# Forming the lower halves of weight tiles by accumulating transfers, with sums moved from GpSimd to VectorE and some casts kept in program order

## The chip, the core and the metric

The kernel runs on one core of one Trainium2 chip. The metric is the device time of one execution in microseconds (us). The engines are named as in the profile: PE is TensorE (PEld its weight loads), DVE is VectorE, ACT is ScalarE, POOL is GpSimd, SP is SyncE. An instruction waits in its engine's queue, and whatever is behind it on that engine waits with it.

## What is computed

One decoder layer on 512 tokens of width 2048, in float32. Cut to what matters:

```python
h = rmsnorm(x, norm1_g)
z = h @ w_in                       # 2048 x 5120: conv value | conv gate | q | k | v
conv_out = conformer_conv(z[..., :2048], conv_w, conv_b, conv_ln_g, conv_ln_b)
#   a * sigmoid(gate), 31 depthwise taps along the tokens, LayerNorm over 1024 channels, silu
o = diff_attention(q, k, v, lam)   # 8 heads, two 64-wide softmaxes each, their difference times v
attn_out = rmsnorm(o, subln_g) * (1.0 - lam_init)
x = x + concatenate([conv_out, attn_out]) @ w_out
h = rmsnorm(x, norm2_g)
x = x + (silu(h @ w_gate) * (h @ w_up)) @ w_down     # 2048 -> 5632 -> 2048
out = rmsnorm(x, final_g)
```

## The kernel before

**Halves.** A product of float32 matrices is made from three products of a rounded type (fp32r). Each operand a is split into an upper half, a rounded to fp32r, and a lower half, what the rounding left. `mm3` (L193 to L197) then adds upper x upper, upper x lower and lower x upper into one PSUM bank. In the profile the three products are L195, L196 and L197; for the gate and up matrices they are L666 to L668.

**Steps.** The weights come as tiles of 128 x 1024 floats (512 KB), one for each step. A step has 24 products of 512 columns. Steps 0 to 31 are the four conv groups, 32 to 47 make v, 48 to 79 are four groups of q and k, 80 to 111 are `w_out`. Then 176 steps of gate and up follow (`split_gu`, 42 products of 256 columns each, by a seven-product block scheme), and 80 steps of `w_down` with a tail. For each step `ensure` issues the load of the tile three steps ahead (tile `raw`, 3 buffers, SP's queue, L183) and the split of the tile two steps ahead.

**The split.** `split_w` calls `split` (L176 to L178): ACT copies `raw` into `wh` (L177, which rounds), and DVE subtracts, `wl` = `raw` - `wh` (L178). Both tiles have 3 buffers, so the buffer of step j is free when PE is done with step j - 3.

**Work beside the steps.** A list `at` holds what is called at the start of a given step (attention: `scores`, `transpose_a`, `attend` and `transpose_o` for 8 heads over steps 56 to 87, and `mix_split`, which splits a tile of the mixed output). `later(n, f)` enters f there, n steps ahead. A queue `bg` holds pieces of DVE work with a price each, the 31 conv taps per channel tile above all; each step earns a credit (`STEP_US` = 4.6 for the narrow steps), the price of other DVE work is taken from it (`split_w` takes 1.15), and pieces of `bg` are issued while it lasts. A scheduler then orders the instructions of each engine by its own estimate; calls wrapped in `keep` stay in program order among themselves.

**Sums.** `add_sum` (L338) adds the eight conv tiles, and `ln_center` squares on ACT (L172) and adds on POOL through `add_square` (L173); all squares share one buffer `sq`. `wout_post` adds the residual (L562) and at once issues a POOL store of it to DRAM (L563).

**From gate and up to down.** `gu_post` empties seven PSUM banks (ACT copies at L678 to L684, DVE at L679 to L683). The product of both is kept in DRAM and comes back by POOL transfers (`reload_hid`, L731); `split_hid` (L736, L737) then casts and subtracts it. The tiles of block 0 lie in slots named b, those of block 1 in slots named a. The first `w_down` step needs the banks that `gu_post` empties.

Of the kernel before, what the change touches and what calls it, by code (L numbers as in the profile page):

```python
# [10 lines left out]
F32R = mybir.dt.float32r  # L11
I32 = mybir.dt.int32
AF = mybir.ActivationFunctionType
# [3 lines left out]
P = 128  # L17
# [19 lines left out]
MIX0 = 80  # L37
STEP_US, GU_STEP_US = 4.6, 5.0
LN_WAIT = 3

C_G1, C_G2, C_GF, C_CB, C_LG, C_LB, C_SG, C_CW = 0, 16, 32, 48, 56, 64, 72, 73
NPAR = C_CW + CT * CK
# [3 lines left out]
def decoder_layer(ctx: ExitStack, tc, xT, w_in, w_out, w_gu, w_dn, par, lamv, out):  # L46
# [14 lines left out]
    def r32(ap):  # L61
        return ap.bitcast(F32)
# [120 lines left out]
        nc.sync.dma_start(t, src)  # L183
        return t

    def split_w(t):
        wh = wts.tile([P, 1024], F32R, tag="wh", bufs=3, name="wh")
        wl = wts.tile([P, 1024], F32R, tag="wl", bufs=3, name="wl")
        split(wh, wl, t)
        credit[0] -= 1.15  # L190
        return wh, wl

    def mm3(acc, ah, al, bh, bl, first, last):  # L193
# [11 lines left out]
    def later(n, f):  # L205

        at[now[0] + n].append(f)
# [90 lines left out]
    def conv_post(g):  # L298
        def post(accs):
            credit[0] -= 3.6  # L300
            value, gate = [], []
            for i in range(2):
                value.append(slotB((36 if g < 3 else 8) + 2 * g + i))
                nc.vector.tensor_tensor(value[i], accs[i], rB[0], op=ALU.mult)
            for i in range(2):
                gate.append(slotB(24 + i))
                nc.vector.tensor_tensor(gate[i], accs[2 + i], rB[0], op=ALU.mult)
                nc.scalar.activation(gate[i], gate[i], AF.Sigmoid)
            for i in range(2):
                ct = 2 * g + i  # L310
                av = value[i]
                nc.vector.tensor_tensor(av, av, gate[i], op=ALU.mult)
                cacc[ct] = slotB(ct)

                def tap(d, ct=ct, h=av):

                    j = CK - 1 - d
                    w = pp[:, C_CW + ct * CK + j : C_CW + ct * CK + j + 1]
                    c = cacc[ct]
                    if d == 0:  # L320
                        b = pp[:, C_CB + ct : C_CB + ct + 1]
                        keep(nc.vector.tensor_scalar(c, h, w, b, op0=ALU.mult, op1=ALU.add))
                    else:
                        keep(
                            nc.vector.scalar_tensor_tensor(  # L325
                                c[:, d:], h[:, : S - d], w, c[:, d:], op0=ALU.mult, op1=ALU.add
                            )
                        )

                for j in range(CK):  # L330
                    bg.append((0.65, lambda j=j, tap=tap: tap(j)))

                def add_sum(ct=ct):
                    if ct == 1:
                        csum[0] = sum_tile()
                    if ct >= 1:
                        prev = cacc[0] if ct == 1 else csum[0]
                        nc.gpsimd.tensor_tensor(csum[0], prev, cacc[ct], op=ALU.add)  # L338

                bg.append((0.0, add_sum))  # L340
            if g == 3:
                bg.append((0.0, lambda: later(LN_WAIT, ln_mean)))

        return post
# [4 lines left out]
    def ln_mean():  # L349
        b = t_bank()  # L350
        nc.tensor.matmul(b, lhsT=ones, rhs=csum[0], start=True, stop=True)
        lnm[0] = slotB(46)
        nc.scalar.activation(lnm[0], b, AF.Copy, scale=1.0 / CW)
        csum[0] = None
        for ct in range(CT):
            bg.append((0.6, lambda ct=ct: ln_center(ct)))
        bg.append((0.0, lambda: later(LN_WAIT, ln_rstd)))

    def ln_center(ct):
        keep(nc.vector.tensor_tensor(cacc[ct], cacc[ct], lnm[0], op=ALU.subtract))  # L360
        csum[0] = add_square(nc.gpsimd, csum[0], cacc[ct])

    def ln_rstd():
        rt = small.tile([P, TB], F32, name="rtln", tag="rtln")
# [192 lines left out]
    def wout_post(cb):  # L557
        def post(accs):
            for f in range(4):
                kt = cb * 4 + f  # L560
                r = xres[kt]
                nc.vector.tensor_tensor(r, accs[f], r, op=ALU.add)  # L562
                nc.gpsimd.dma_start(x2_kept[kt], r)  # L563
                ssum2[0] = add_square(nc.vector, ssum2[0], r)
            if cb == 3:
                later(3, finish_rms2)

        return post
# [42 lines left out]

    chunk = [0]

    def split_gu(t):


        c = chunk[0]
# [115 lines left out]

    def split_hid(b, k):
        hi, lo = hid_halves[b, k]
        nc.scalar.copy(hi, r32(lo))  # L736
        nc.vector.tensor_tensor(lo, r32(lo), r32(hi), op=ALU.subtract)  # L737

    def dn_post(cb):
        def post(accs):  # L740
# [72 lines left out]
    for kt in range(KT):  # L813
        at[d0 - 2 + kt].append(lambda kt=kt: reload_x2(kt))
    n_main = len(steps)

    LOAD_AHEAD, SPLIT_AHEAD = 3, 2
    raws, halves = {}, {}
# [3 lines left out]
    def ensure(i, cut=True):  # L822
        for j in range(len(raws), min(i + LOAD_AHEAD + 1, len(srcs))):
            raws[j] = load(srcs[j])
        if cut:
            for j in range(len(halves), min(i + SPLIT_AHEAD + 1, len(srcs))):
                halves[j] = (steps[j][3] if j < n_main else split_w)(raws[j])

    for n in range(2):
        load_xT(2 * n)  # L830
# [248 lines left out]
```

## Time and profile before

| what | us |
|---|---|
| median of 3 runs | 2098.47 |
| the runs | 2096.27, 2098.47, 2098.81 |
| profiled execution, its own time | 2096.77 |
| its span, first to last instruction | 2095.0 |
| PE busy in it | 2062.4 |
| DVE busy | 1551.6 |
| ACT busy | 869.1 |
| POOL busy | 140.2 |

The span lies inside the profiled execution's own time and is 1.8 us shorter. "Busy" of PE is the union of matmuls that overlap: one of 512 columns is shown with 389 ns while the next starts some 230 ns later, so a short stop of PE need not show as idle time. The granted clock is given per stretch, 1.00 being the higher of TensorE's two levels (2.4 GHz).

### The profile page before, as it was taken

What the parts mean: (1) busy time and instruction counts of PE and PEld (TensorE: products, weight loads), DVE (VectorE), ACT (ScalarE), POOL (GpSimd) and SP (SyncE); (2) the same over time, 40 slices, a digit from 0 to 9 for tenths busy, and PEclk for the clock granted to TensorE, in tenths of its full rate; (3) what the DMA queues carried; (4) which work ended last, traced back from release to release, by engine and by line L of the source; (5) the groups of instructions that cost most, each with busy time, mean ns of one, the idle gap of its engine ahead of it and who ended that gap; (6) DMA issues with size and microseconds to landing.
All of it is one profiled execution on the core that took longest, in us unless ns stands there. A gap on an engine that the chain in (4) does not pass through costs nothing.

```text
span 2095.0 us, 32883 instructions
## 1 busy us (share of the span) xinstructions
PE 2062.4 (98%) x12852; PEld 1859.1 (89%) x12852; DVE 1551.6 (74%) x2698; ACT 869.1 (41%) x1458; POOL 140.2 (7%) x194
## 2 busy tenths in 40 slices
PE   8999999999999999999999999999999999999997
PEld 7888887777788999999999999999998888888887
DVE  7999998888754889888988988998988334232244
ACT  5222225667543554444444444444455223212133
POOL 4000000200000000000000000000013001000004
PEclk9999999999999999999999999999999999999998
DMA  5232332224233333333433333333357234322332
GB/s 206 91 101 91 101 100 72 70 71 136 96 113 118 118 114 121 122 111 105 138 111 112 122 121 117 119 123 117 107 181 278 99 121 141 101 96 95 101 111 81
DMA packets 71531, 243.59 MB, mean 116 GB/s; under 512 B 8784, under 2 KB 9296, under 8 KB 71376
## 3 DMA queue, kind: packets, MB, share of 16 engines
q1 hardware_dynamic: 61776, 210.04, 30.1%
q0 software_dynamic: 9600, 31.46, 4.4%
q8 instruction: 100, 1.64, 0.3%
q14 instruction: 55, 0.45, 0.1%
HBM read 221.54 MB, written 19.92 MB: 115 GB/s over the span
## 4 chain that ended last, share of the span: by engine, by line
PE 87%; issue 5%; DVE 4%; ACT 1%; DMA 1%; POOL 0%; SPq 0%; DVEq 0%; POOLq 0%; ACTq 0%
PE k L195 15%; PE k L196 15%; PE k L197 15%; PE k L666 13%; PE k L667 13%; PE k L668 13%; PE k L509 1%; DVE wl L178 1%; PE k L459 1%; DVE a L278 0%; PE k L460 0%; DVE b L435 0%; PE k L498 0%; DMA a<-hid 0%; DMA raw<-w_gu_dram 0%
## 5 line engine op out<-in xcount | busy, mean ns | idle before, releaser
L178 DVE TENSOR_TENSOR wl<-raw,wh 128x1024 fp32r<-128x1024 f32 (+1 forms) x196 | 243.7, 1244 | 315.8 <-ACT wh L177 315.1
L177 ACT CAST wh<-raw 128x1024 fp32r<-128x1024 f32 (+1 forms) x196 | 204.5, 1043 | 564.7 <-PE k L196 485.0
L195 PE MATMUL k<-a,wh 128*128 128x512 f32 (+1 forms) x992 | 386.2, 391 | 4.4 <-ACT wh L177 1.9
L197 PE MATMUL k<-a,wl 128*128 128x512 f32 (+1 forms) x992 | 386.9, 390 | 2.4 <-DVE wl L178 2.4
L196 PE MATMUL k<-a,wh 128*128 128x512 f32 (+1 forms) x992 | 386.6, 390 | 0.0
L637 ACT CAST b<-b 128x512 fp32r<-128x512 f32 x176 | 109.3, 621 | 291.3 <-PE k L667 245.5
L195 PEld LDWEIGHTS k<-a,wh 128*128 128x128 f32 x992 | 187.6, 189 | 42.1 <-ACT wh L177 2.6
L197 PEld LDWEIGHTS k<-a,wl 128*128 128x128 f32 x992 | 187.4, 189 | 40.3 <-DVE wl L178 3.7
L196 PEld LDWEIGHTS k<-a,wh 128*128 128x128 f32 x992 | 187.6, 189 | 36.9 <-issue 0.5
L668 PE MATMUL k<-b,b 128*128 128x256 f32 x704 | 199.6, 284 | 0.0
L666 PE MATMUL k<-b,b 128*128 128x256 f32 x704 | 199.4, 283 | 0.1
L666 PE MATMUL k<-a,b 128*128 128x256 f32 x704 | 199.2, 283 | 0.0
L667 PE MATMUL k<-a,b 128*128 128x256 f32 x704 | 199.2, 283 | 0.0
L668 PE MATMUL k<-a,b 128*128 128x256 f32 x704 | 199.2, 283 | 0.0
L667 PE MATMUL k<-b,b 128*128 128x256 f32 x704 | 199.2, 283 | 0.0
L325 DVE SCALAR_TENSOR_TENSOR b<-b,pp,b 128x511 f32<-128x511 f32 (+14 forms) x240 | 179.9, 750 | 6.4
L195 PE MATMUL k<-b,wh 128*128 128x512 f32 x448 | 175.7, 392 | 3.5 <-ACT a L678 3.5
L196 PE MATMUL k<-b,wh 128*128 128x512 f32 x448 | 175.3, 391 | 0.0
L197 PE MATMUL k<-b,wl 128*128 128x512 f32 x448 | 175.2, 391 | 0.0
L639 DVE TENSOR_TENSOR wl<-raw,wh 128x768 fp32r<-128x768 f32 x176 | 167.0, 949 | 2.0 <-ACT wh L628 1.9
L629 DVE TENSOR_TENSOR b<-raw 128x512 f32<-128x512 f32 x176 | 119.4, 686 | 54.7 <-DMA raw<-w_gu_dram 53.3
L628 ACT CAST wh<-raw 128x768 fp32r<-128x768 f32 x176 | 146.8, 834 | 23.3 <-PE k L667 6.0
(207 smaller groups left out, 4682.0 us busy)
## 6 DMA issues: line engine op xcount, KB each, us to landing
raw<-w_gu_dram SPq DMA_DIRECT2D x176, 512.0 KB, 3.3
raw<-w_down_dram SPq DMA_DIRECT2D x88, 512.0 KB, 3.2
raw<-w_qk_dram SPq DMA_DIRECT2D x32, 512.0 KB, 3.2
raw<-w_out_dram SPq DMA_DIRECT2D x32, 512.0 KB, 3.2
raw<-w_conv_dram SPq DMA_DIRECT2D x30, 512.0 KB, 3.3
hid<-b POOLq DMA_DIRECT2D x44, 256.0 KB, 3.1
b<-xT_dram SPq DMA_DIRECT2D x32, 256.0 KB, 3.9
raw<-w_v_dram SPq DMA_DIRECT2D x16, 512.0 KB, 3.3
```

Source lines behind the costliest of these rows:

```text
L177: nc.scalar.copy(hi, src)
L178: nc.vector.tensor_tensor(lo, src, r32(hi), op=ALU.subtract)
L195: nc.tensor.matmul(acc, lhsT=ah, rhs=bh, start=first, stop=False)
L196: nc.tensor.matmul(acc, lhsT=ah, rhs=bl, start=False, stop=False)
L197: nc.tensor.matmul(acc, lhsT=al, rhs=bh, start=False, stop=last)
L325: nc.vector.scalar_tensor_tensor(c[:, d:], h[:, : S - d], w, c[:, d:], op0=ALU.mult, op1=ALU.add)
L628: nc.scalar.copy(wh[:, pure], t[:, pure])
L629: nc.vector.tensor_tensor(t13.rearrange("p (i c) -> p i c", i=2), t[:, a].unsqueeze(1).to_broadcast([P, 2, 256]), t[:, 256:768].rearrange( ...
L639: nc.vector.tensor_tensor(wl[:, pure], t[:, pure], r32(wh[:, pure]), op=ALU.subtract)
L666: nc.tensor.matmul(acc, lhsT=qh[:, cut], rhs=sh, start=first, stop=False)
L667: nc.tensor.matmul(acc, lhsT=qh[:, cut], rhs=sl, start=False, stop=False)
L668: nc.tensor.matmul(acc, lhsT=ql[:, cut], rhs=sh, start=False, stop=last)
```

## The change

For steps 8 to 95 the split is replaced by `split_add`: ACT writes the negated upper half into `wl`, a POOL transfer reads the same weights from DRAM once more and adds them onto `wl`, and ACT writes the upper half into `wh`. DVE has no part in it. Both split functions now get the source as well. The conv sums and the LayerNorm sums of squares go from POOL to DVE with a price in `bg`; the stores of the residual are issued two steps later; the cast and the subtraction of reloaded tiles are kept in program order. `split_add` takes nothing from the credit.

```diff
+ADD0, ADD1 = 8, 96
-    def split_w(t):
+    def split_w(t, src):
         wh = wts.tile([P, 1024], F32R, tag="wh", bufs=3, name="wh")
         wl = wts.tile([P, 1024], F32R, tag="wl", bufs=3, name="wl")
         split(wh, wl, t)
         credit[0] -= 1.15
         return wh, wl
+    def split_add(t, src):
+        wh = wts.tile([P, 1024], F32R, tag="wh", bufs=3, name="wh")
+        wl = wts.tile([P, 1024], F32R, tag="wl", bufs=3, name="wl")
+        nc.scalar.activation(wl, t, AF.Copy, scale=-1.0)
+        nc.gpsimd.dma_start(wl, src, accum_op=ALU.add)
+        nc.scalar.copy(wh, t)
+        return wh, wl
...
-                        nc.gpsimd.tensor_tensor(csum[0], prev, cacc[ct], op=ALU.add)
-                bg.append((0.0, add_sum))
+                        nc.vector.tensor_tensor(csum[0], prev, cacc[ct], op=ALU.add)
+                bg.append((0.6, add_sum))
...
-            bg.append((0.6, lambda ct=ct: ln_center(ct)))
+            bg.append((1.2, lambda ct=ct: ln_center(ct)))
...
-        csum[0] = add_square(nc.gpsimd, csum[0], cacc[ct])
+        csum[0] = add_square(nc.vector, csum[0], cacc[ct])
...
-                nc.gpsimd.dma_start(x2_kept[kt], r)
+                later(2, lambda kt=kt, r=r: nc.gpsimd.dma_start(x2_kept[kt], r))
...
-    def split_gu(t):
+    def split_gu(t, src):
...
-        nc.scalar.copy(hi, r32(lo))
-        nc.vector.tensor_tensor(lo, r32(lo), r32(hi), op=ALU.subtract)
+        keep(nc.scalar.copy(hi, r32(lo)))
+        keep(nc.vector.tensor_tensor(lo, r32(lo), r32(hi), op=ALU.subtract))
...
+    for n in range(ADD0, ADD1):
+        steps[n] = (*steps[n][:3], split_add)
...
-                halves[j] = (steps[j][3] if j < n_main else split_w)(raws[j])
+                halves[j] = (steps[j][3] if j < n_main else split_w)(raws[j], srcs[j])
```

The order of instructions moves at three places. The numbers in the names are those of slots and buffers; lines of the changed kernel lie 1 to 12 further down than before (L195 to L197 are L205 to L207, L534 is L544, L678 is L688, L736 is L746).

**ACT in the conv steps.** Before:

```order
L177 CAST wh_778<-raw_740 128x1024
L177 CAST wh_813<-raw_776 128x1024
L177 CAST wh_848<-raw_811 128x1024
L177 CAST wh_883<-raw_846 128x1024
L308 ACTIVATE b24_915<-b24_915 128x512
```

In the changed kernel:

```order
L200 CAST wh_753<-raw_713 128x1024
L198 ACTIVATE wl_754<-raw_713 128x1024
L200 CAST wh_790<-raw_751 128x1024
L198 ACTIVATE wl_791<-raw_751 128x1024
L200 CAST wh_828<-raw_788 128x1024
L198 ACTIVATE wl_829<-raw_788 128x1024
```

Each cast is followed by the negation of the same tile; on POOL the transfer that adds onto it (L199) stands alone in the queue for 82 rows, with no other work between.

**PE at the last head.** L534 (L544) is the transposition of the last head's output in `transpose_o(7)`; a15 and a31 are the halves that `mix_split` makes of it. Before:

```order
L197 MATMUL k3_4498<-a14_4892,wl_4949 128x512
L534 MATMUL k7_5022<-ident_77,b39_4898 128x128 x4
L195 MATMUL k0_4495<-a15_5029,wh_4948 128x512
L195 MATMUL k1_4496<-a15_5029,wh_4948 128x512
L195 MATMUL k2_4497<-a15_5029,wh_4948 128x512
```

In the changed kernel the transposition stands here, and the first product that reads a15 stands 23 rows below it:

```order
L206 MATMUL k0_4570<-a29_4732,wh_4959 128x512
L544 MATMUL k7_5103<-ident_77,b39_4977 128x128 x4
L207 MATMUL k0_4570<-a13_4731,wl_4960 128x512
L205 MATMUL k1_4571<-a12_4498,wh_4959 128x512
L206 MATMUL k1_4571<-a28_4499,wh_4959 128x512
L207 MATMUL k1_4571<-a12_4498,wl_4960 128x512
```

It has moved from directly ahead of the products that need its result to a whole run of products earlier.

**ACT at the change from gate and up to down.** L678 (L688) copies the bank k0 that the first `w_down` step writes; L736 (L746) are the casts of reloaded tiles. Before:

```order
L736 CAST a3_18308<-a19_18309 128x512
L736 CAST a4_18345<-a20_18346 128x512
L177 CAST wh_17806<-raw_17748 128x1024
L736 CAST a5_18386<-a21_18387 128x512
L678 COPY a14_17862<-k0_17333 128x512
```

In the changed kernel:

```order
L746 CAST b36_17713<-b37_17714 128x512
L746 CAST b38_17716<-b39_17717 128x512
L746 CAST b40_17719<-b41_17720 128x512
L746 CAST b42_17722<-b43_17723 128x512
L688 COPY a14_17950<-k0_17421 128x512
L690 COPY a15_17951<-k7_17449 128x512
```

No cast of an a slot stands ahead of the copy any more; those of block 1 begin 21 rows behind it, and those of block 0 (slots b) stand later than before. On ACT the loads of its function table go from 11 to 6: the LayerNorm's silus (L380) now stand in one row ahead of the first softmax (L472) and no longer between softmaxes.

## Rows read from the trace of the kernel before

**Rows 1.** The page, engines: busy us (share of the span), instructions.

```profile
PE 2062.4 (98%) x12852; PEld 1859.1 (89%) x12852; DVE 1551.6 (74%) x2698; ACT 869.1 (41%) x1458; POOL 140.2 (7%) x194
```

**Rows 2.** Stretches: us, busy of each engine (instructions), granted clock, DMA share, GB/s.

```profile
60.00:300.00 240.00, 240.00 (x1061) 198.72 (x1060) 227.26 (x289) 55.61 (x59) 8.58 (x6) 1.00 0.29 97
300.00:460.00 160.00, 154.83 (x750) 124.80 (x749) 134.06 (x323) 87.53 (x189) 12.81 (x8) 1.00 0.22 73
460.00:540.00 80.00, 78.85 (x400) 63.38 (x400) 69.74 (x183) 59.58 (x132) 0.00 (x0) 1.00 0.37 119
540.00:580.00 40.00, 36.03 (x165) 28.93 (x164) 29.86 (x80) 21.28 (x50) 2.35 (x4) 0.91 0.30 98
1560.00:1600.00 40.00, 36.47 (x277) 35.30 (x276) 33.19 (x56) 23.45 (x40) 20.35 (x38) 0.93 0.92 324
```

**Rows 3.** Waits of PE, 300 to 580 us: us in total, times, longest.

```profile
PE k L534 <- DVE b L528: 3.3, 2, 2.5
PE k L459 <- ACT b L472: 2.0, 1, 2.0
PE k L195 <- ACT a L177: 1.5, 1, 1.5
```

**Rows 4.** Timeline of PE at the last head: start, us, instruction [idle before, releaser].

```profile
562.90 0.66 PE L534 MATMUL k<-ident,b 128*128 128x128 f32 x4 [2.47 <-DVE b L528]
565.05 2.07 PE L195 MATMUL k<-a,wh 128*128 128x512 f32 x4 [1.49 <-ACT a L177]
566.92 0.63 PE L196 MATMUL k<-a,wh 128*128 128x512 f32 x1
...
570.33 0.40 PE L195 MATMUL k<-a,wh 128*128 128x512 f32 x1
570.56 0.40 PE L196 MATMUL k<-a,wh 128*128 128x512 f32 x1
```

**Rows 5.** Timeline of PE at the first down step.

```profile
1595.34 0.80 PE L195 MATMUL k<-b,wh 128*128 128x512 f32 x1 [3.53 <-ACT a L678]
...
1601.05 0.43 PE L196 MATMUL k<-b,wh 128*128 128x512 f32 x1
```

**Rows 6.** Timeline of ACT there.

```profile
1592.72 0.62 ACT L736 CAST a<-a 128x512 fp32r<-128x512 f32 x1 [2.58 <-DMA a<-hid]
...
1594.71 0.58 ACT L678 COPY a<-k 128x512 f32<-128x512 f32 x1
```

**Rows 7.** DVE by line, 300 to 580 us: count, busy us, mean ns, idle before.

```profile
L178 DVE TENSOR_TENSOR wl<-raw,wh 128x1024 fp32r<-128x1024 f32 x38 | 46.3, 1218 | 3.2 <-ACT wh L177 2.8
...
L173 DVE TENSOR_TENSOR sum<-sum,sq 128x512 f32<-128x512 f32 x3 | 2.1, 685 | 0.0
```

**Rows 8.** ACT by line, 300 to 580 us.

```profile
L472 ACT ACT_TABLE_LOAD x4 | 5.1, 1283 | 0.1
...
L380 ACT ACT_TABLE_LOAD x3 | 3.8, 1283 | 0.1
```

**Rows 9.** ACT by line and form, 0 to 60 us.

```profile
L277 ACT ACTIVATE a<-b,pp 128x512 fp32r<-128x512 f32 x16 | 10.8, 714 | 2.3 <-DMA b<-xT_dram 2.3
...
L177 ACT CAST wh<-raw 128x512 fp32r<-128x512 f32 x4 | 2.4, 610 | 0.7 <-DMA raw<-w_conv_dram 0.7
```

**Rows 10.** ACT by line, 60 to 300 us.

```profile
L177 ACT CAST wh<-raw 128x1024 fp32r<-128x1024 f32 x44 | 46.4, 1055 | 168.3 <-PE k L196 95.7 <-PE k L197 52.0 <-issue 11.8
```

**Rows 11.** DMA, 60 to 300 us: packets, MB, share; issues with median us to landing.

```profile
q1 hardware_dynamic: 6336, 23.07, 29.1%
...
raw<-w_conv_dram SPq DMA_DIRECT2D x19, 512.0 KB, 3.2
```

**Rows 12.** DMA issues, 1560 to 1600 us.

```profile
b<-x POOLq DMA_DIRECT2D x16, 256.0 KB, 6.6
```

**Rows 13.** The page, DMA issues of the whole span.

```profile
hid<-b POOLq DMA_DIRECT2D x44, 256.0 KB, 3.1
```

**Rows 14.** Timeline of POOL before the longest wait for a softmax.

```profile
408.63 1.26 POOL L173 TENSOR_TENSOR sum<-sum,sq 128x512 f32<-128x512 f32 x1 [0.74 <-ACT sq L172]
```

## Prediction

> **What bounds the kernel now.** I read the page first: PE is busy for 2062 of 2095 us [rows 1]. A change that leaves the products alone can only win back the stretches in which PE stands still or runs at its lower level, and can lose whatever it makes PE wait. The table of stretches says where those are [rows 2]. From 60 to 300 us (conv and v) PE is never idle, although DVE is busy for 227 of 240 us. It has 44 casts of a weight tile, one per step [rows 10], so a step takes 240 / 44 = 5.45 us there: PE's own pace. From 300 to 460 us PE is idle for 5.2 us and from 460 to 540 for 1.2; DVE is busy for 84% and 87%, ACT for 55% and 74%. From 540 to 580 us 4.0 us are idle and the mean clock is 0.91, and from 1560 to 1600 us 3.5 us are idle at a mean clock of 0.93. These four stretches are all that this change can win from. The waits of PE name what ended last in attention: DVE twice with 3.3 us in all, and ACT's exponentials once with 2.0 [rows 3].
>
> **Part 1: the last head.** PE waits 2.47 us for DVE before the transposition of the last head and 1.49 us for ACT's cast behind it [rows 4]. After that it runs at its lower level: the four products from 565.05 take 1.87 us and the eight from 566.92 to 570.33 take 3.41, 0.43 each, where the next two start 0.23 us apart. At 0.23 the twelve would take 2.8 us, so the clock costs 2.5 us and the place 6.5 in all. In the changed order 23 products stand between this transposition and the first product that needs it, 23 x 0.23 = 5.3 us of cover, against 2.15 us from transposition to product before. What can stay is the wait ahead of the transposition, which now comes earlier. Bounds: 2 to 6.5 us gained; I take 5, since the cover is over twice the chain.
>
> **Part 2: attention.** DVE loses 38 subtractions of 1.22 us between 300 and 580 us, 46 us [rows 7], and the taps that ran there come earlier, since nothing is charged for the split. POOL's adds, behind which ACT's squares and then an exponential stood, go from 1.26 us [rows 14] to 0.685 on DVE [rows 7]. ACT loads its table five times less, 5 x 1.28 = 6.4 us [rows 8]. Against this ACT gets a negation per step. Its price is not in the trace; a scaled activation of 512 columns takes 0.71 us and a cast 0.61 [rows 9], a cast of 1024 takes 1.06 [rows 10], so it lies between 1.06 and 1.06 x 0.71 / 0.61 = 1.23, and I take 1.2. With 38 steps in 280 us a step here takes 7.4 us, so ACT's load from 300 to 460 us becomes 87.5 + 22 x 1.2 = 114 of 160 us, and from 460 to 540 us 59.6 + 11 x 1.2 = 73 of 80, less the table loads. The stops shown are 6.3 us in all; a stop shows only behind the 0.16 us by which one matmul's row overlaps the next, so the full loss is above it, up to some 10 us for twenty-odd stops. Bounds: 0 to 10 gained; I take 6, because DVE, the releaser of the largest share, is the engine that is relieved.
>
> **Part 3: from gate and up to down.** PE stands 3.53 us for the copy that empties the first bank [rows 5], and that copy stood in ACT's queue behind a cast that waited 2.58 us for a reload [rows 6]. Then thirteen products take 1601.05 - 1595.34 = 5.7 us where 13 x 0.23 = 3.0 would do: 2.7 us at the lower level, 6.2 in all. With the casts in program order no cast of block 1 is ahead of the copy, and the bank is complete after the first six products of the last gate-and-up step, so the copy can be done before PE ends. Bounds: 3 (if block 0's later casts delay it) to 6.2; I take 5.5.
>
> **Part 4: is the lower half there in time?** The buffer of a step comes free when PE ends the step three earlier; ACT's cast waits for just that, 168 us over 44 casts [rows 10]. Cast and negation take 1.06 + 1.2 = 2.3 us, the transfer follows, and PE wants the lower half at its third product, two steps and two products later: 10.9 + 0.46 = 11.4 us. So the transfer has 9.1 us from issue to landing. A plain load of 512 KB lands in 3.2 us [rows 11], of which it occupies all 16 DMA queues for 29.1% x 240 / 44 = 1.59 us; the other 1.6 is fixed. A transfer that adds is in no row. From below it costs one load; from above three (read both operands, write one, nothing overlapped), 4.8 us. I take two, 3.2 us: the nearest row is the load of the same bytes, and a second operand of the same size is read. It lands after 1.6 + 3.2 = 4.8 us, or 6.4 with the load that is issued beside it. Even 1.6 + 4.8 + 1.6 = 8.0 is inside 9.1. POOL's own transfers land in 3.1 us on a quiet queue [rows 13] and in 6.6 where the queues are 92% busy [rows 12, 2].
> The trace has no adding transfer, and the Trainium skill, Collectives: The Full Stack, section "The bandwidth ceiling: the fold count and why AG ≠ RS ≠ AR", gives a price: an add needs two source reads and so runs at half the rate of a copy. By that page alone it would occupy the queues for two loads' time, an estimate that gives the sum below; no run here shows it yet.
> The queues are then busy for 1.59 + 3.2 = 4.8 of 5.45 us, 88%. Two places on ACT leave less than 9.1 us: around steps 57 and 58, where eight silus and twelve half casts of 0.6 to 0.7 us stand ahead of two negations, and around step 90, where the first blocks of gate and up do. I take 1.5 us for each, 3 us lost; bounds 0 to 8. Behind a late negation stand that step's transfer on POOL and, on ACT, the next exponentials.
>
> **Part 5: what comes at nothing.** Fourteen adds go from POOL to DVE: 14 x 0.685 = 9.6 us [rows 7], covered by the 88 x 1.22 = 107 us that DVE loses. Without that cover they would sit in the tap queue, which PE doesn't wait for between 60 and 300 us. The stores of the residual are issued two steps later so that POOL doesn't stand for DVE ahead of the adding transfers; nobody reads them for a thousand us.
>
> **The sum.** -5 - 6 - 5.5 + 3 = -13.5 us. Against the profiled execution (2096.77 us, span 2095.0) that is 2083.3; the median of the runs shown is 1.7 us above it, 2098.47, so 2085.0. The ends of the terms give -6.5 - 10 - 6.2 = -22.7 and -2 - 0 - 3 + 8 = +3: 2076 to 2101 for this case.
>
> **Rivals.** (a) The DMA queues become the bound, which decides from 5.45 - 1.59 = 3.86 us, 2.4 loads, per adding transfer. At three loads each short step takes 1.59 + 4.77 = 6.36 us, 0.91 more; the 56 short steps (8 to 55 and 88 to 95) lose 51 us, the attention steps of 7.4 us nothing: 2085 + 51 = 2136. For it: no row has this transfer, and where the queues are 92% busy a small POOL transfer takes twice its time. Against it: only the top of my bounds reaches it. (b) ACT's queue: cast and negation are due at the start of a step, where the exponentials want to go, and each exponential waits in line. If the score chain of the 32 attention steps is longer by one negation each, 32 x 1.2 = 38 us, part 2 is void, and parts 1 and 3 remain: 2098.5 + 38 - 10.5 + 3 would be 2129; half of the steps give 2110. It decides from the step in which chain and negation exceed 7.4 us. For it: ACT at 91% from 460 to 540 us. Against it: the subtractions that leave DVE stood in the same chain with 1.22 us each. (c) PE's stops only change their releaser: parts 1 to 3 at their low ends, part 4 near its high one, 2098.5 - 5 + 6 = about 2099.
>
> **How the numbers follow.** A difference of 0.2% (4 us) is about what a measurement of this kernel can tell from none. Forecast case 64%, (a) 14%, (b) 8%, (c) 12%, others 2%. In the forecast case 61 of the 64 are faster by over 0.2%, with one more from elsewhere: faster 0.62. Within 0.2%: 2 of the forecast and 11 of (c), 0.13. Slower: (a), (b) and rests, 0.25. The range reaches from the good end of the terms, 2075, to half-way past (b), 2126; it leaves out (a) and some 5%. The forecast case alone has 2076 to 2101.
>
> **What would show it.** The profile after should show PE with less than 1 us idle at the last head and at the first down step, both at clock 1.00; a step of 5.45 us still, from 60 to 300 us, with the DMA share near 0.88; adding transfers landing in 5 to 7 us; DVE's load from 300 to 540 us some 40 us lower and ACT's 35 higher. A share near 1.00 with PE waiting for `wl` in each conv step would be (a); PE waiting for ACT's exponentials in most attention steps would be (b). The forecast is wrong if the adding transfer takes over 9 us to land or over 3.9 us of the queues.

## The result, and the profile after

The changed kernel takes 2080.78 us (median of 4 runs, 2078.82 to 2081.82) against 2098.64 us for the kernel before, measured beside it (4 runs): ratio 0.9915, 95% interval 0.9898 to 0.9932. That is 17.9 us less, and inside the forecast range. Its profiled execution took 2081.82 us, with a span of 2079.9 us.

The engines' row of its page, which answers to [rows 1] (busy us, share of the span, instructions):

```profile
PE 2054.6 (99%) x12852; PEld 1855.1 (89%) x12852; DVE 1460.8 (70%) x2624; ACT 942.1 (45%) x1541; POOL 194.1 (9%) x268
```

The stretches of [rows 2] in the changed kernel (us, busy of PE, PEld, DVE, ACT, POOL, granted clock, DMA share, GB/s). The last one is set 15 us earlier than before, because the first down step now comes 14 us earlier:

```profile
60.00:300.00 240.00, 239.13 (x1052) 196.87 (x1051) 206.53 (x291) 101.88 (x112) 38.13 (x44) 1.00 0.86 190
300.00:460.00 160.00, 157.81 (x776) 130.07 (x775) 99.96 (x289) 113.12 (x224) 19.91 (x23) 1.00 0.71 158
460.00:540.00 80.00, 79.86 (x416) 66.13 (x415) 59.24 (x184) 59.60 (x137) 8.64 (x10) 1.00 0.76 179
540.00:580.00 40.00, 39.74 (x184) 32.58 (x184) 18.31 (x49) 24.86 (x43) 8.29 (x11) 1.00 0.84 198
1545.00:1585.00 40.00, 40.00 (x321) 39.39 (x321) 37.48 (x63) 23.48 (x41) 17.98 (x34) 1.00 0.87 309
```

Idle time of PE from 300 to 460 us falls from 5.2 to 2.2 us, at the last head from 4.0 to 0.3, at the first down step from 3.5 to none, and the clock is 1.00 at both places, where it was 0.91 and 0.93. From 300 to 540 us DVE has 44.6 us less work, and ACT 25.6 more. What is new is the 0.9 us that PE stands between 60 and 300 us.

The waits of PE in the changed kernel, 60 to 600 us (us in total, times, longest), where [rows 3] had 3.3, 2.0 and 1.5 us:

```profile
PE k L205 <- DVE b L435: 0.8, 1, 0.8
PE k L508 <- DVE b L496: 0.7, 2, 0.3
PE k L206 <- DMA wl<-w_v_dram: 0.6, 1, 0.6
...
PE k L207 <- DMA wl<-w_conv_dram: 0.3, 1, 0.3
```

The timeline of PE at the last head, against [rows 4], and at the first down step, against [rows 5]:

```profile
548.77 0.66 PE L544 MATMUL k<-ident,b 128*128 128x128 f32 x4 [0.24 <-DVE b L538]
549.18 0.48 PE L207 MATMUL k<-a,wl 128*128 128x512 f32 x1
...
1581.43 0.40 PE L205 MATMUL k<-b,wh 128*128 128x512 f32 x1
1581.67 0.40 PE L206 MATMUL k<-b,wh 128*128 128x512 f32 x1
```

The transposition waits 0.24 us for DVE instead of 2.47; nothing behind it waits, up to step 88 and beyond. The first two down products start 0.24 us apart, at the higher level.

**Where the time went.** The timeline of PE gives the start of each step: its first product is every 24th of the three product lines. Gate and up have lines of their own and are not counted, so here they lie between the starts of steps 111 and 112, and step 112 is the first down step. Differences of such starts, in us:

| steps | before | after | difference |
|---|---|---|---|
| 8 to 46 (conv, v) | 212.16 | 213.75 | +1.6 |
| 47 to 87 (v's end, attention, last head) | 299.39 | 286.01 | -13.4 |
| 88 to 112 (rest of `w_out`, gate and up, first down step) | 1033.31 | 1027.86 | -5.4 |

What is left of the 15.1 us between the spans lies in the first eight steps (+0.5) and in the tail (+1.6). The starts of single steps mislead in one place: steps 47 to 55 take 2.7 us longer than before, but not because PE waits. The LayerNorm's twelve float32 products, 2.9 us of work, now stand there:

```profile
L361 PE MATMUL k<-sum,ones 128*128 128x512 f32 x2 | 1.0, 592 | 0.0
L148 PE MATMUL k<-sq,ones 128*128 128x512 f32 x2 | 1.0, 592 | 0.0
L159 PE MATMUL k<-ones_cw,sum 128*128 128x1 f32 x8 | 0.9, 239 | 0.0
```

These are PE's groups between 273 and 331 us (count, busy us, mean ns, idle before). Before, the same twelve came between 331 and 460 us:

```profile
L147 PE MATMUL k<-sq,ones 128*128 128x512 f32 x2 | 1.1, 644 | 0.4 <-ACT junk L521 0.4
L351 PE MATMUL k<-sum,ones 128*128 128x512 f32 x2 | 1.1, 630 | 0.0
L158 PE MATMUL k<-ones_cw,sum 128*128 128x1 f32 x8 | 1.0, 249 | 0.0
```

So a stretch is only compared fairly if it holds the same work, and steps 47 to 87 are taken as one below. A second caution: gate and up alone, from the first of their products to the last, take 889.3 to 894.4 us in the kernels below, and what follows step 112 takes 490.8 to 493.5, though most edits lie far from both. Differences of one or two us in the last column of the next table are not assigned to a cause.

### The profile page after: what moved, and what is told of

It is laid out like the page before. It is cut to its first block, busy times and chain, and to the rows that moved or that the text cites. A ratio compares the mean times of both kernels' runs of the same rounds, so it can differ in the third digit from the quotient of the medians.

```text
span 2079.9 us, 33053 instructions
## 1 busy us (share of the span) xinstructions
PE 2054.6 (99%) x12852; PEld 1855.1 (89%) x12852; DVE 1460.8 (70%) x2624; ACT 942.1 (45%) x1541; POOL 194.1 (9%) x268
## 4 chain that ended last, share of the span: by engine, by line
PE 85%; issue 7%; DVE 3%; POOL 1%; ACT 1%; DMA 1%; SPq 0%; DVEq 0%; POOLq 0%; ACTq 0%
PE k L206 14%; PE k L207 14%; PE k L205 14%; PE k L676 14%; PE k L677 14%; PE k L678 14%; POOL wl L199 1%; PE k L519 1%; DMA raw<-w_gu_dram 0%; DVE a L288 0%; PE k L470 0%; DMA wl<-w_v_dram 0%; PE k L469 0%; DVE b L445 0%; PE k L508 0%
## 5 line engine op out<-in xcount | busy, mean ns | idle before, releaser
L205 PE MATMUL k<-a,wh 128*128 128x512 f32 (+1 forms) x992 | 385.4, 389 | 3.2 <-ACT wh L178 1.8
L207 PE MATMUL k<-a,wl 128*128 128x512 f32 (+1 forms) x992 | 383.7, 387 | 2.7 <-DVE wl L179 2.4
L179 DVE TENSOR_TENSOR wl<-raw,wh 128x1024 fp32r<-128x1024 f32 (+1 forms) x108 | 134.3, 1244 | 319.0 <-ACT wh L178 319.0
L178 ACT CAST wh<-raw 128x1024 fp32r<-128x1024 f32 (+1 forms) x108 | 112.0, 1037 | 365.0 <-PE k L206 355.2
L647 ACT CAST b<-b 128x512 fp32r<-128x512 f32 x176 | 109.2, 621 | 268.4 <-PE k L677 232.1
L205 PEld LDWEIGHTS k<-a,wh 128*128 128x128 f32 x992 | 186.4, 188 | 41.8 <-ACT wh L178 2.4
L207 PEld LDWEIGHTS k<-a,wl 128*128 128x128 f32 x992 | 186.4, 188 | 41.1 <-DVE wl L179 3.7
L676 PE MATMUL k<-b,b 128*128 128x256 f32 x704 | 200.2, 284 | 0.9 <-DVE b L693 0.7
L678 PE MATMUL k<-b,b 128*128 128x256 f32 x704 | 199.6, 283 | 0.0
L676 PE MATMUL k<-a,b 128*128 128x256 f32 x704 | 199.2, 283 | 0.0
L678 PE MATMUL k<-a,b 128*128 128x256 f32 x704 | 199.2, 283 | 0.0
L205 PE MATMUL k<-b,wh 128*128 128x512 f32 x448 | 174.3, 389 | 0.0
L207 PE MATMUL k<-b,wl 128*128 128x512 f32 x448 | 174.3, 389 | 0.0
L648 ACT CAST b<-b 128x512 fp32r<-128x512 f32 x176 | 109.1, 620 | 120.2 <-DVE b L646 95.8
```

Source lines behind the costliest of these rows:

```text
L178: nc.scalar.copy(hi, src)
L179: nc.vector.tensor_tensor(lo, src, r32(hi), op=ALU.subtract)
L205: nc.tensor.matmul(acc, lhsT=ah, rhs=bh, start=first, stop=False)
L207: nc.tensor.matmul(acc, lhsT=al, rhs=bh, start=False, stop=last)
L647: nc.scalar.copy(h13, t13)
L676: nc.tensor.matmul(acc, lhsT=qh[:, cut], rhs=sh, start=first, stop=False)
```

## The experiments

The theory at the start was the prediction's: attention gains because DVE loses its subtractions there, the first down step because of the kept casts, and late lower halves give some of it back. The rivals were the earlier taps, the sums on DVE, and the transfer's own load. All runs are in one table (us; the ratio is to the kernel before on the same chip, the stretches are from one profiled execution each):

| kernel | median | ratio, 95% | steps 8-46 | 47-87 | 88-112 |
|---|---|---|---|---|---|
| before | 2098.64 | | 212.2 | 299.4 | 1033.3 |
| after | 2080.78 | 0.9915 (0.9898-0.9932) | 213.8 | 286.0 | 1027.9 |
| kept casts alone | 2090.81 | 0.9962 (0.9950-0.9975) | 212.2 | 299.3 | 1026.3 |
| all but the kept casts | 2090.60 | 0.9963 (0.9949-0.9977) | 213.8 | 286.0 | 1035.2 |
| transfers in 56-95 only | 2078.33 | 0.9904 (0.9890-0.9917) | 212.2 | 285.8 | 1028.3 |
| transfers in 8-55 only | 2081.43 | 0.9918 (0.9905-0.9932) | 212.9 | 285.6 | 1027.6 |
| sums and stores alone | 2093.57 | 0.9978 (0.9969-0.9986) | 212.2 | 295.0 | 1034.2 |
| after, sums on POOL | 2090.47 | 0.9963 (0.9950-0.9975) | 213.9 | 293.6 | 1028.1 |
| no transfers, split uncharged | 2094.24 | 0.9982 (0.9972-0.9991) | 226.6 | 287.2 | 1029.3 |
| after, negation first | 2089.28 | 0.9957 (0.9945-0.9969) | 214.4 | 290.8 | 1030.8 |
| 56-95 only, negation first | 2088.66 | 0.9955 (0.9942-0.9967) | 212.2 | 294.6 | 1027.7 |
| no transfers in 46-57 | 2079.01 | 0.9911 (0.9897-0.9924) | 212.3 | 284.7 | 1025.5 |
| plain transfers | 2079.92 | 0.9918 (0.9904-0.9931) | 212.2 | 286.0 | 1027.8 |
| each addition twice | 2302.68 | 1.0972 (1.0954-1.0991) | 329.9 | 365.2 | 1053.3 |

**The kept casts, alone and taken away.** To the kernel before only this was done, and in the changed kernel only this undone:

```diff
-        nc.scalar.copy(hi, r32(lo))
-        nc.vector.tensor_tensor(lo, r32(lo), r32(hi), op=ALU.subtract)
+        keep(nc.scalar.copy(hi, r32(lo)))
+        keep(nc.vector.tensor_tensor(lo, r32(lo), r32(hi), op=ALU.subtract))
```

> The kernel before with one part of the change alone: the casts and subtractions of reloaded tiles kept in program order. Theory: the stop at the first down step (3.5 us of idle and 2.7 us at the lower clock level before; together 5.4 us in the difference of the two traces) goes with this part alone, so 2098.6 - 5.4 = 2093.2 us, ratio 0.9974, and the two products-of-down stretches look as in the changed kernel. Rival: the stop is gone in the changed kernel because PE arrives there at another moment relative to the reloads (POOL's queue, the stores moved by two steps), then this part alone gives 2098.6 and PE waits there still, for another cast or for the reload itself.

> The changed kernel without that part: the casts of reloaded tiles where the scheduler puts them. Theory: loses what the part gives, 2080.8 + 5.4 = 2086.2 us, with PE waiting some 3 us for the bank's copy again. Rival: 2080.8.

Alone it gains 7 us by the medians and 7.1 in steps 88 to 112; taken away it costs 9.8 by the medians and 7.3 there. In the first kernel ACT's timeline has the copy L678 done 2.1 us before PE's first down product, which starts at 1591.06 us:

```profile
1588.41 0.58 ACT L678 COPY a<-k 128x512 f32<-128x512 f32 x1
```

The second kernel's waits of PE, 1540 to 1600 us, and ACT's timeline there: a cast of an a slot stands ahead of the copy again and waits for its reload.

```profile
PE k L205 <- ACT a L688: 5.6, 1, 5.6
```

```profile
1582.56 0.62 ACT L746 CAST a<-a 128x512 fp32r<-128x512 f32 x1 [2.54 <-DMA a<-hid]
1583.08 1.04 ACT L178 CAST wh<-raw 128x1024 fp32r<-128x1024 f32 x1
...
1584.55 0.58 ACT L688 COPY a<-k 128x512 f32<-128x512 f32 x1
```

The theory holds and the rival falls. The price is larger than I took. In the second kernel that is in part because its stop is longer than the one of the kernel before, 5.6 us against 3.5 [rows 5], so what it loses is not the price of the same stop.

**Transfers in one half of the steps only.**

```diff
-ADD0, ADD1 = 8, 96
+ADD0, ADD1 = 56, 96
```

> The changed kernel with the adding transfers only in steps 56 to 95; the conv and v steps (8 to 55) split on DVE as before. Theory: what the changed kernel gains lies in the attention steps, whose subtractions leave DVE, and at the last head, and the conv and v steps only lose (the steps 26, 34, 47, 48, 52, 53 and 54 take 4.2 us longer than before, where an adding transfer lands late): 2080.8 - 4.2 = 2076.6 us, ratio 0.9895 to the kernel before. Rival: the gain in attention comes from the taps and the LayerNorm sums that run earlier because the conv steps are charged nothing for their split; then attention gives back some 8 us and the result is 2084 to 2085.

and with `8, 56`:

> The changed kernel with the adding transfers only in steps 8 to 55; from step 56 on the split is DVE's as before. Theory (relief of DVE within attention is what counts): the conv steps' loss of 4.2 us stays, attention gains nothing, the last head gains some 2 us because its transposition stands only 7 products ahead of its reader here, the first down step gains 5.4: 2098.6 + 4.2 - 2 - 5.4 = 2095.4 us. Rival (the earlier taps count): attention keeps its 8 us and the last head part of its 8, about 2081 to 2087.

Both gave the whole gain of steps 47 to 87: 285.8 and 285.6 us, where both halves together give 286.0. So my theory (only the subtractions that leave attention count) fell, and so did its rival (only the earlier taps count): either is enough. The stretch from 300 to 460 us, in the two kernels in this order:

```profile
300.00:460.00 160.00, 157.83 (x778) 129.54 (x776) 128.05 (x332) 114.41 (x224) 18.30 (x21) 1.00 0.64 140
```

```profile
300.00:460.00 160.00, 159.69 (x785) 130.11 (x784) 118.87 (x309) 94.04 (x199) 1.73 (x2) 1.00 0.32 94
```

DVE has 128 and 119 us there, against 134 before [rows 2] and 100 with both. The reliefs add up on DVE and not on PE, and the busy time of DVE does not tell what they are worth: in the first kernel it is only 6 us lower, and PE has the whole gain. PE's waits tell it better. From 60 to 600 us those that name DVE add up to 5.2 us before, and to 2.0 and 0.2 us in these two kernels. That more relief buys nothing because the score chain then no longer stands behind DVE is argued, not shown. Both kernels also have the sums on DVE.

**The sums alone, and the sums back on POOL.** The first is the kernel before with these lines, the second the changed kernel without the first two:

```diff
-nc.gpsimd.tensor_tensor(csum[0], prev, cacc[ct], op=ALU.add)
+nc.vector.tensor_tensor(csum[0], prev, cacc[ct], op=ALU.add)
-csum[0] = add_square(nc.gpsimd, csum[0], cacc[ct])
+csum[0] = add_square(nc.vector, csum[0], cacc[ct])
-nc.gpsimd.dma_start(x2_kept[kt], r)
+later(2, lambda kt=kt, r=r: nc.gpsimd.dma_start(x2_kept[kt], r))
```

> The kernel before with one part alone: the conv sums and the sums of squares added on DVE, at the prices of before, and the residual's stores two steps later; no adding transfers, no kept order of casts. Adding transfers in attention alone and adding transfers in the conv steps alone both won most of attention's time (steps 56 to 86 took 231.3 and 228.2 us, against 236.6 before and 228.9 with both), and both have the sums on DVE. Theory: what wins is DVE's relief, by its own subtractions that go or by taps that are done before attention starts, either being enough; then this kernel gains little, 2096 to 2098.5 us, and steps 56 to 86 take 235 us or more. Rival: what wins in attention is that ACT's squares and exponentials no longer stand behind POOL's adds; then steps 56 to 86 take about 229 to 231 us here too and step 87 less than 13.8, and the time is 2083 to 2091 us.

> The changed kernel with those sums back on POOL, all else and the prices as in the change. Theory (DVE's relief by the subtractions is what wins): attention keeps its gain, and the fourteen adds of 1.26 us that now stand in POOL's queue ahead of adding transfers, each waiting for DVE or ACT, cost some late lower halves: 2081 to 2085 us. Rival (the sums are what wins): attention and the last head give back up to 16 us, 2090 us or more.

Alone, with the residual's stores two steps later, they win 4.4 us in steps 47 to 87 (between the two expectations: steps 56 to 86 took 232.3 us), and the last head stays as it was; the waits of PE from 300 to 590 us still begin so:

```profile
PE k L534 <- DVE b L528: 2.5, 1, 2.5
```

The exponential's 2.0 us of [rows 3] is not among them. With the transfers the sums play another part: put back on POOL they cost 9.7 us by the medians, 7.6 of it in steps 47 to 87, because an add that waits for DVE then holds an adding transfer behind it (POOL's timeline):

```profile
270.70 1.28 POOL L348 TENSOR_TENSOR sum<-sum,b 128x512 f32<-128x512 f32 x1 [10.08 <-DVE b L335]
271.94 0.87 POOL L199 DMA_DIRECT2D wl<-w_v_dram  x1
```

PE waits 3.1 us for that one. From step 56 to 86 this kernel takes 228.9 us, just as the changed one, so beside the transfers attention does not need the sums on DVE. The loss is over twice what the theory's upper end allowed; its kind was right.

**Without any adding transfer.** `ADD0, ADD1 = 0, 0`, and the charge of the DVE split dropped in the early steps:

```diff
-        credit[0] -= 1.15
+        credit[0] -= 0.0 if now[0] < 56 else 1.15
```

> The changed kernel without any adding transfer: every step splits on DVE, but the split of steps 0 to 55 is charged nothing, as in the kernel with adding transfers in the conv steps only (2081.4 us); sums on DVE and kept casts as in the change. It asks whether the transfers are needed or only the taps' earlier place. Theory (the transfers are what makes room for the early taps): DVE was busy for 207 us between 60 and 300 us with the transfers; with 44 subtractions of 1.22 us it would need 261 of 240 us, so PE waits for lower halves, some 20 us are lost there and no time is won in all: 2095 to 2105 us, with PE waiting for wl from DVE. Rival (the charge alone does it): the taps slide into the first attention steps without PE's waiting, attention and the last head keep their 16 us, and the time is 2076 to 2082 us.

Steps 47 to 87 gain 12.2 us without any transfer, by the earlier taps and the sums on DVE, but steps 8 to 46 lose 14.4. The waits of PE from 60 to 300 us, and the stretch:

```profile
PE k L206 <- DVE wl L179: 9.4, 3, 4.9
```

```profile
60.00:300.00 240.00, 230.61 (x997) 189.35 (x996) 233.28 (x314) 52.60 (x57) 0.00 (x0) 0.98 0.27 90
```

DVE is full (233 of 240 us) and PE waits for its subtractions. The theory holds, with a loss some 6 us smaller than I had set, so that the median lies 0.8 us below its range. What this kernel still wins over the kernel before, 4.3 us, is less than the kept casts alone win. The early taps are worth the time only where something makes room on DVE.

**The negation ahead of the cast.** In `split_add`:

```diff
-        nc.scalar.activation(wl, t, AF.Copy, scale=-1.0)
+        keep(nc.scalar.activation(wl, t, AF.Copy, scale=-1.0))
         nc.gpsimd.dma_start(wl, src, accum_op=ALU.add)
-        nc.scalar.copy(wh, t)
+        keep(nc.scalar.copy(wh, t))
```

> The changed kernel with the negation kept ahead of the cast of the same tile on ACT, as the code is written; the scheduler puts the cast first, so that each adding transfer starts 1.05 us later than it could. Theory (in the late steps 26, 34, 47, 48, 52 to 54, 56 and 58, which cost 6 us, ACT stands behind a sigmoid or a silu and the transfer then lands 0.3 to 1 us too late): 1.05 us earlier removes most of it, 2080.8 - 4 = 2076.8 us, and PE no longer waits for an adding transfer between 60 and 320 us. Rival: the loss comes from elsewhere (the DVE's conv work or the queues' load), and the time stays at 2080.8, or the later casts cost as much.

> Adding transfers in steps 56 to 95 only, and the negation ahead of the cast. Theory: with the conv steps at PE's own pace there is little late to win, 2077 to 2078.3 us (2078.3 without the order). Rival: the negation put between the score chain's casts and exponentials delays those, and attention gives back 2 us or more: 2080 or above.

They lost 8.5 and 10.3 us by the medians, where I expected gains of 4 and of up to 1.3. The kept order makes the pair go as one, and where much stands ahead of it, transfers are late and then bunched. In the first kernel (POOL's timeline, then the row of PE's with the longest wait):

```profile
297.90 0.86 POOL L199 DMA_DIRECT2D wl<-w_qk_dram  x1 [7.71 <-ACT wl L198]
299.80 0.87 POOL L199 DMA_DIRECT2D wl<-w_qk_dram  x1 [1.03 <-ACT wl L198]
```

```profile
304.83 0.80 PE L207 MATMUL k<-a,wl 128*128 128x512 f32 x1 [2.56 <-DMA wl<-w_qk_dram]
```

In the changed kernel these two are issued at 293.32 and 298.37 us: there the negation of the first stands between two squares that wait for DVE, here behind all of them. In the second kernel, with transfers in 56 to 95 only, PE waits 3.69 us at once, until 474.46 us, for this transfer (POOL's timeline):

```profile
466.26 0.86 POOL L199 DMA_DIRECT2D wl<-w_qk_dram  x1 [8.96 <-ACT wl L198]
```

Without the kept order the same step's transfer is issued at 456.59 us. Here ACT did not wait: from 456 to 466.3 us it is busy for 10.24 of 10.30 us, with exponentials, casts, silus and two table loads ahead of the negation. So what decides when a transfer starts is what stands ahead of the negation on ACT, waiting in the first kernel and at work in the second, and not the 1.05 us of the cast.

**No transfers around the LayerNorm.**

```diff
-    for n in range(ADD0, ADD1):
+    for n in [*range(8, 46), *range(58, 96)]:
```

> The changed kernel without adding transfers in steps 46 to 57, where DVE splits as before: the stretch in which squares on ACT wait for DVE and negations stand behind them. Theory (late lower halves there are the change's own loss): steps 47 to 55 take 5.44 us each again (2.8 us less) and steps 56 to 59 some 28 instead of 30.0 us; with all else as in the change 2080.8 - 4.5 = 2076 us. Rival: the subtractions that are back on DVE delay the LayerNorm's sums by 12 x 1.22 us and with them the first softmaxes; then attention gives back as much, 2080 to 2083 us.

The median, 2079.01, cannot be told from the changed kernel's or from that of transfers in 56 to 95 only (the intervals overlap). Steps 47 to 55 take 51.7 us as in the changed kernel, so this part of the theory fell: it is the LayerNorm's work shown above. Steps 56 to 59 take 28.7 us instead of 30.0, where the theory had some 28. The 2.4 us that this execution wins in steps 88 to 112 lie far from the edit: four short stops of 0.14 to 0.23 us of PE behind DVE (L676 for L693) that the changed kernel has between 1098 and 1464 us are not there, which is 0.8 us of it. The rest is open, and this execution is the fastest of the four of its kernel, 3 us below their median.

**A transfer that doesn't add.**

```diff
-        nc.gpsimd.dma_start(wl, src, accum_op=ALU.add)
+        nc.gpsimd.dma_start(wl, src)
```

> The changed kernel with the accumulating transfers replaced by plain transfers from GpSimd's queue that write over the tile: the addition is left out, so that the lower halves are whole weights; the order of all instructions is the same. Theory (an addition occupies the queues 1.8 times as long as a plain load of the same bytes, 3.0 against 1.66 us, and that is why halves come late behind bunched issues): DMA share from 60 to 300 us falls from 0.86 to about 0.61, the transfers land in some 5 us instead of 7.0 to 8.3, and of the 6 us that the late steps cost 3 or more go: 2076 to 2078 us. Rival: the late steps come from ACT's order alone and stay: 2080.8 us.

The DMA rows from 60 to 300 us of the changed kernel and then of this one (queue, packets, MB, share; issues, KB, median us to landing):

```profile
q0 software_dynamic: 6249, 22.73, 55.4%
q1 hardware_dynamic: 6221, 22.67, 30.5%
wl<-w_conv_dram POOLq DMA_DIRECT2D x22, 512.0 KB, 7.7
raw<-w_v_dram SPq DMA_DIRECT2D x16, 512.0 KB, 6.6
wl<-w_v_dram POOLq DMA_DIRECT2D x16, 512.0 KB, 7.0
```

```profile
q0 software_dynamic: 6261, 22.83, 28.5%
q1 hardware_dynamic: 6336, 23.07, 28.2%
wl<-w_conv_dram POOLq DMA_DIRECT2D x22, 512.0 KB, 4.6
...
wl<-w_v_dram POOLq DMA_DIRECT2D x16, 512.0 KB, 3.8
```

An addition occupies the 16 queues for 0.554 x 240 / 44 = 3.02 us, the plain transfer of the same bytes for 0.285 x 240 / 44 = 1.55: 1.94 times, and it lands some 3.1 us later. PE no longer stands between 60 and 300 us, but that is 1.6 us in steps 8 to 46 and nothing else: 47 to 87 are the same to 0.04 us. So the whole of what the slow landing costs this kernel is 1.6 us, about half of the least that the theory gave, and the medians (2079.92 and 2080.78 us) cannot be told apart; the wait at L435 around step 56 (0.8 us, DVE) stays as well.

**Each addition twice.**

```diff
         nc.gpsimd.dma_start(wl, src, accum_op=ALU.add)
+        nc.gpsimd.dma_start(wl, src, accum_op=ALU.add)
```

> The changed kernel with each adding transfer issued twice: the weights are added two times, so that the lower halves are whole weights again. It puts the queues past the point from which the prediction's rival (a) decides. Theory (the queues are then the bound, 1.66 + 2 x 3.02 = 7.7 us per step): the 48 steps 8 to 55 and the eight steps 88 to 95 take 7.7 us instead of 5.45, 56 x 2.25 = 126 us more, and the attention steps of 7.2 us lose 0.5 us each, 16 us: about 2080.8 + 142 = 2223 us, at a DMA share near 1.00. Rival (the transfers overlap better under load than their sum, or the issue on POOL of 0.86 us each is no cost): 2150 us or less; or the second addition waits for the first's landing, 7 to 8 us later, and a short step takes 15.5 / 2 us or more: 2230 us and above at a DMA share well below 1.

Steps 8 to 55 take 8.45 us each, and the time lies above the 2223 us of the theory. The DMA share from 60 to 466 us is 0.87, not 1.00, and POOL's timeline shows the third outcome named, that the second addition waits for the first's landing:

```profile
161.66 0.86 POOL L200 DMA_DIRECT2D wl<-w_conv_dram  x1 [6.63 <-DMA wl<-w_conv_dram]
162.19 1.22 POOL L199 DMA_DIRECT2D wl<-w_conv_dram  x1
169.93 0.86 POOL L200 DMA_DIRECT2D wl<-w_conv_dram  x1 [6.52 <-DMA wl<-w_conv_dram]
```

POOL sends the second of one tile and the first of the next together and stands until that has landed: one pair per 8.3 us. So this run does not show where the queues become the bound; it shows that a chain of landings decides before they do.

## Why the prediction came out as it did

**The sum** was -13.5 us and the medians moved by -17.9. The profiled executions, against which the sum was made, moved by 15.0 (2096.77 to 2081.82); in the tail, behind step 112, where of the change only the kept casts remain, the second of them runs 1.6 us longer. That the sum came within 1.5 us of this is in part luck. The three gains are larger than forecast, 19.9 us against 16.5, and the late lower halves cost 1.6 instead of 3; against that stand 3.2 us that are in no term: 1.1 in gate and up, 1.6 in the tail and 0.5 in the first eight steps.

**Parts 1 and 2** were to give 5 and 6 us; steps 47 to 87, which hold both, gave 13.4, inside their bounds of 2 and 16.5. The places were right: but for 0.24 us the last head runs without a stop, at clock 1.00, and the waits of [rows 3] are gone or below 1 us.

At the last head PE's timeline has 10.3 us in the kernel before from its last product ahead of the transposition (560.03 us) to the start of step 88 (570.33). At the higher level the same products take 3.4 us (0.23 for each of the 13, some 0.4 for the transposition), so the place cost 6.9; some 0.4 of it is left after. That is 6.5 us for part 1, its upper bound, and 6.9 for part 2. Two things changed at once there: the transposition stands further ahead of its reader, and DVE's result for it comes earlier, 4.8 us ahead of the start of step 87 (553.60 us) instead of 6.4 us behind it (556.51). With transfers in 8 to 55 only, the transposition stands 7 products ahead of its reader instead of 23, directly ahead of step 87; PE stops for 0.22 us ahead of it, and step 87 takes 5.75 us. So long a cover was not needed. No run moves the transposition or DVE's result alone.

The reason given for part 2 was wrong in how it put its causes together. I named DVE's lost subtractions, the earlier taps, the adds that leave POOL and ACT's table loads side by side, and took 6 us because DVE is relieved. The runs show that the first two do not add up: the lost subtractions suffice (transfers in 56 to 95 only), and the taps' earlier place suffices without them (transfers in 8 to 55 only), each beside the sums on DVE, whose move alone is worth 4.4 us. The table loads are not needed for it: in the former of these kernels silus still stand in two groups between softmaxes, and it gains as much. ACT's load from 300 to 460 us came as forecast (113 us for 114), but from 460 to 540 us it is 59.6 us, as before, where I had 73 less the table loads: besides those, the silus have moved out of that stretch.

**Part 3** had the right mechanism and too small a size. From the start of the last gate-and-up product to the start of the second down step the kernel before takes 12.1 us, and the changed kernel and the one with the kept casts alone take 5.6 each. That is 6.5 us at the place, where I took 5.5 with an upper bound of 6.2. Of the 7.1 us that the kept casts alone win, the other 0.5 lie in gate and up. The changed kernel has the same 6.5 at the place, but its gate and up takes 1.1 us longer than before, PE standing for 0.8 us in the four short stops named above, and so steps 88 to 112 gain 5.4.

**Part 4** was right in its arithmetic's outcome and wrong in its places. The negation takes 1.055 us, like the cast (I took 1.2, with 1.06 the lower bound):

```profile
L198 ACT ACTIVATE wl<-raw 128x1024 fp32r<-128x1024 f32 x44 | 46.4, 1055 | 47.5 <-PE k L206 47.5
L200 ACT CAST wh<-raw 128x1024 fp32r<-128x1024 f32 x44 | 46.0, 1045 | 70.9 <-issue 66.5 <-PE k L206 2.8 <-PE k L207 1.5
```

The addition's price, taken as two loads or 3.2 us, is 3.02, and the DMA share is 0.86 where 0.88 was forecast. The Trainium skill, Collectives: The Full Stack, section "The bandwidth ceiling: the fold count and why AG ≠ RS ≠ AR", has, for collectives, an add at half the rate of a copy for its two source reads; by that rule it is two, and the trace agrees with 1.94. The landing was mis-sized: 7.0 to 7.7 us in the conv and v steps instead of 4.8 to 6.4, and the plain loads beside them land in 5.5 to 6.6 instead of the 3.2 of [rows 11]. The two transfers' times on the queues, which I had added, do not give this; why is open. By these medians it is still inside the 9.1 us allowed; the slowest of the 88, issued at 208.98 us, took 9.7, and PE shows no stop for it. The lateness that I put at steps 57, 58 and 90 (3 us) came at steps 26 and 34 (0.6 and 0.9 us), where I had seen none. ACT's, POOL's and PE's rows for the first:

```profile
147.13 0.64 ACT L318 ACTIVATE b<-b 128x512 f32<-128x512 f32 x1 [4.22 <-DVE b L317]
147.67 1.04 ACT L200 CAST wh<-raw 128x1024 fp32r<-128x1024 f32 x1
148.61 1.05 ACT L198 ACTIVATE wl<-raw 128x1024 fp32r<-128x1024 f32 x1
```

```profile
149.96 0.86 POOL L199 DMA_DIRECT2D wl<-w_conv_dram  x1 [5.89 <-ACT wl L198]
```

```profile
158.11 0.50 PE L207 MATMUL k<-a,wl 128*128 128x512 f32 x1 [0.29 <-DMA wl<-w_conv_dram]
```

A sigmoid stood 4.22 us for DVE, the negation behind it, and the transfer came too late for PE. In the prediction I looked for places where ACT is busy; in the changed kernel the place was one where it waits. Steps 88 to 95 take 43.5 us, as before.

**Part 5** held in its time and not in its words. No run shows the adds costing anything on DVE, but the sums' move is no mere companion: it wins 4.4 us in steps 47 to 87 alone, and without it the changed kernel is 9.7 us slower.

**The rivals.** (a) does not come about: an addition is 1.9 loads, and the point was 2.4; whether that point is right the run with two additions doesn't tell, since landings bound it first. (b) does not either: in the changed kernel no wait of PE from 60 to 600 us names ACT. With the negation bound to the cast and transfers in 56 to 95 only, steps 47 to 87 lose 9 us, but that is not (b): PE's waits from 60 to 600 us name adding transfers with 5.0 us and ACT's exponentials (L482) with 0.2. (c) is refuted by the clean rows at both places.

## What to carry to other kernels

Relief of one engine that comes from two sides is worth what the waiting engine lost, once: measure each side alone before both are paid for. In this kernel a transfer that completes an engine's work started when that engine had done what stood ahead of it; where it was late, the engine was once waiting (4.22 us behind DVE) and once busy (10.24 of 10.30 us), so both kinds of place have to be looked for. A move of side work between queues (the sums off POOL) can be what half of the main edit's gain hangs on.

## What the runs showed of the hardware

A transfer from GpSimd's queue that adds onto the tile in float32 took 3.02 us of the 16 queues per 512 KB, 1.94 times a plain one, landed 3.1 us later, and its issue kept POOL busy for longer. POOL's groups from 60 to 300 us, the changed kernel and then the one with plain transfers:

```profile
L199 POOL DMA_DIRECT2D wl<-w_v_dram x16 | 13.8, 864 | 73.2 <-ACT wl L198 73.2
```

```profile
L199 POOL DMA_DIRECT2D wl<-w_v_dram x16 | 8.4, 528 | 77.6 <-ACT wl L198 77.6
```

0.86 against 0.53 us. The bytes that the trace counts are the same in both (22.7 and 22.8 MB), so the GB/s column, 190 and 192, doesn't show the addition; the share does.
